# Five single moves in the instruction order of a retention and HGRN2 step

## The chip, the cores and the metric

The kernel runs on one core of a Trainium2 chip. The metric is the time of one execution in device microseconds, as the median of several runs.

## What is computed

One inference step of a hybrid decoder layer (depth 1): a prompt of 2048 tokens and eight decode rows of one token each, model width 1024. The normalised input is projected by w_in into eight groups of 512 columns; four of them feed a retention branch, four an HGRN2 branch. Each branch has four heads of 128 and runs a chunked recurrence; the outputs are normalised, gated and projected by w_out.

```
h = rmsnorm(x, norm_g)
p = h @ w_in
rq, rk, rv, rg, hq, hf, hi, hgate = split(p, 8)
# retention: rotary on rq, rk; fixed decay per head
o_ret, s_ret_new = chunked_decay_recurrence(rq, rk, rv, log_gamma, s_ret)
o_ret = head_rmsnorm(o_ret, ret_g) * silu(rg)
# HGRN2: forget gate from hf, key from 1 - gate
o_hg, s_hg_new = chunked_decay_recurrence(silu(hq), kin, hi, logf, s_hg)
o_hg = head_rmsnorm(o_hg, hg_g) * silu(hgate)
y = x + concat(o_ret, o_hg) @ w_out      # then the final rmsnorm
```

It returns the normalised y of the prompt and of the decode rows, and the new states of both branches for both.

## The kernel before

All large products are made from two parts of each operand, a high and a low one, with three matmuls (`three`, L348: high times high, high times low, low times high). The parts are made on chip: ACT (ScalarE) writes the high part, DVE (VectorE) the difference, both at L117 and L118 (`hi_lo`).

**Three main stages follow each other.** In the first, 24 token pairs (`v_pair(i, after)`, L383) run in three sets of eight. In each pair, a matrix product of blocks is made from seven smaller products (CHAIN, L355: A11·B11, A12·B21, S2·T2, S1·T1, S3·T3, S4·B22, A22·T4), each of twelve matmuls into a bank a, b or c; S and T are sums of blocks. The set number m says which weights are used. While set m−1 runs, the weights of set m are read (`wg_load`, at product 0 of pairs j = 2 to 5 of the set), multiplied with the eight decode rows (`wg_decode`, tile pgd, L590), summed to T1 to T4 and stored to memory (`wg_spool`: the sums in `w_sums` are four DVE instructions, the stores four DMAs by SP, SyncE, to ws1T). They are read back at j = 7 (`wg_fetch`) and split into high and low parts (`wg_split`) at the end of that pair and the start of the next one. In the third set the retention recurrence and the retention decode heads run beside the pairs (`r_*`, `d_load`, `d_mul`, `d_add`, `d_mm`): `d_load(hd)` loads a head's state dS and the broadcast values dv.

In the second stage the scan of HGRN2 runs in eight units (a half of the tokens and a head): the projection of a unit (`hgrn_proj`) is interleaved with the recurrence of the one before (`hgrn_rec`), whose steps stand in two lists, `levels` and `rest`, with a number that says at which share of the projection they are issued. `collect` copies the eight decode columns of q, k and f of each unit of the first half (df, dk, dq) and `d_pad(1)` pads the q of the four heads for the decode products (dqp). `side_at` lists steps beside a unit, with the unit's number and the share of it (4.1 is in unit 4).

In the third stage the output projection starts with four plain chunks (`py`, L1657) beside the tail of the last scan unit; the fill list gives each added step its share of the stage. Chunk pairs by seven products follow (`o_pair`); for the first, p0, `op_s12` (L1697) and `op_s34` (L1704) make sums of blocks (oS), `op_a` and `op_s23` split blocks and sums into high and low parts.

**What sets the order.** PE's order is the order in which the matmuls are written: a step in `after[n]` comes behind product n of a pair (0.5 is the middle of product 1). On the other engines a scheduler places the instructions, by their data, so a step that is written later may still be put ahead. `behind(f)` (L126) ties a step behind the last instructions so far of DVE, ACT and SP. All DMAs of the pairs go through SP's queue in its order, so a DMA that waits for data holds those behind it.

**The names in the steps.** pv3c is bank c of pair 3; B22h and B22l are the two parts of B22; wgr is the raw weight of a set; vo, rk, t are tiles of the rotation after a projection (`turn`, L360); pkt is the transpose of rk, par the scores of the retention; rq and rv are loaded from the stores qt_dram and v_dram; pah the scores in the scan; obh the normalised output of a head and poth its transpose; qqh and kh the scan's q and k.

Of the kernel before, what the change touches and what calls it, by code (L numbers as in the profile page):

```python
# [41 lines left out]
def step_kernel(ctx, tc, a, out):  # L42
# [83 lines left out]
    def behind(f):  # L126

        last = {}
        for i in reversed(nc.cur_bb.bb.instructions):
            if i.engine in (dve.engine, act.engine, sp.engine) and i.engine not in last:  # L130
                last[i.engine] = i
                if len(last) == 3:
                    break
        with ExitStack() as es:
            for i in last.values():
                es.enter_context(tc.issue_after(i))
            f()
# [383 lines left out]
    def wg_decode(n, k):  # L521
        if n not in pgd:
            pgd[n] = ps_o.tile([P, 256], F32, tag="o", name=f"pgd{n}")
        for kk in (k, k + 4):
            four(pgd[n], xs[:, kk], wr[kk].rearrange("p a b -> p (a b)"), kk == 0, kk == KT - 1)

    def wg_spool(n, k):
        for op, r in w_sums(wr[k], wr[k + 4]):
            sp.dma_start(w_sums_dram[n][op][:, k], r)
# [42 lines left out]
    def wg_split(op):  # L572
        h, l = Bop[op]
        for n, r in enumerate(wg_raw[op]):
            kk = slice(2 * n, 2 * n + 2)
            hi_lo(h[:, kk], l[:, kk], r)
# [252 lines left out]
    def d_load(hd):  # L829
        ty, h = divmod(hd, NH)  # L830
        S = rawp.tile([P, NB, P], F32, tag="raw", name=f"dS{hd}")
        vb = rawp.tile([P, NB, P], F32, tag="raw", name=f"dv{hd}")
        sp.dma_start(S, (a["state_ret"], a["state_hgrn"])[ty][0, :, h].rearrange("b d v -> d b v"))
        sp.dma_start(vb, vd_dram[ty, :, h * P : (h + 1) * P].partition_broadcast(P))
        dec["l", hd] = (S, vb)
# [19 lines left out]
    def d_pad(ty):  # L855
        if ty:
            x = pools["up"].tile([P, NH, 32], F32, tag="dqp", name="dqp")
        else:
            x = sm.tile([P, NH, 32], F32, tag="old", name="dqr", bufs=1)
        dve.tensor_copy(x[:, :, 8:32], zero.unsqueeze(1).to_broadcast([P, NH, 24]))  # L860
        dve.tensor_copy(x[:, :, 0:8], dq[:, ty * NH : ty * NH + NH])
        dec["q", ty] = x
# [41 lines left out]
    SPLIT_AT = 3  # L904
    for i in range(2, n_tok):
        after = {n: [] for n in range(7)}
        m, j = i // N_V + 1, i % N_V
        if N_V <= i < 2 * N_V:
            after[3.5 if i > N_V + 1 else 4.5 if i > N_V else 5.5] = [q_flip]
        if N_V < i <= 2 * N_V:  # L910
            after.setdefault(2.5 if i < N_V + 3 else 1.5 if i < 2 * N_V else 2, []).append(q_flip)
        if i in (N_V, 2 * N_V):
            after[4 if i == N_V else 1] += [lambda m=i // N_V: wg_decode_turn(m)]
        if i == 2 * N_V:
            r_begin()
        if i >= 2 * N_V:
            for n, f in r_steps(i - 2 * N_V).items():
                after.setdefault(n, []).extend(f)
        if same(i + 1):
            for op in ("S1", "S2", "S3", "S4"):  # L920
                sop[i + 1, op] = sop[i, op]
        elif i + 1 < n_tok:
            if not spooled(i + 1):
                after[1] += [lambda i=i: spread(i + 1)]
            tied = behind if i >= N_V - 1 else lambda f: f()
            late = 2 if same(i) else 0
            after[2 + late] += [
                lambda i=i, t=tied: t(lambda: tok_ops(i + 1)), lambda i=i, t=tied: t(lambda: s_split(i + 1, 0))
            ]
            after[4 + late // 2] += [lambda i=i, t=tied: t(lambda: s_split(i + 1, 1))]  # L930
        if i + 2 < n_tok and not same(i + 2):
            at = 5 if i % N_V > 2 else 2
            if same(i + 1):
                at = 6
            after[at] += [lambda i=i: tok_load(i + 2)]
        if i + 2 < N_V:
            after[1 if i == 2 else 2] += [lambda i=i: behind(lambda: stats_sum(i + 2, 0)), lambda i=i: stats_load(i + 2, 1)]
            after[4] += [lambda i=i: behind(lambda: stats_sum(i + 2, 1)), lambda i=i: stats_end(i + 2)]
            if i + 3 < N_V:
                after[5] += [lambda i=i: stats_load(i + 3, 0)]  # L940
        if N_V <= i + 1 < n_tok:
            after[4] += [lambda i=i: rot_load(i + 1)]
        if i == 2:
            after[3] += [lambda: behind(decode_values_out)]
            after[2] += [decode_spread]
        if m < 3:
            if 2 <= j < 6:
                after[0] += [lambda m=m, k=j - 2: wg_load(m, k)]
                after[4] += [lambda m=m, k=j - 2: wg_decode(m, k), lambda m=m, k=j - 2: wg_spool(m, k)]
            if j == 7:  # L950
                after[0] += [lambda m=m: behind(lambda: wg_decode_out(m))]
                for n, (_, op, _) in enumerate(CHAIN):
                    after[n] = [lambda m=m, op=op: wg_fetch(m, op)] + after[n]
        if i >= N_V - 1 and j in (7, 0) and i < n_tok - 1:
            for n, (_, op, _) in enumerate(CHAIN):
                if (n + SPLIT_AT) // 7 == (j + 1) % N_V:
                    after[3 if n == 6 else (n + SPLIT_AT) % 7] += [lambda op=op: behind(lambda: wg_split(op))]
        if i == 2 * N_V + 2:
            after[0] += [lambda: d_pad(0)]
        hd = i - 2 * N_V - 2  # L960
        if 0 <= hd < NH:
            after[2] += [lambda hd=hd: d_load(hd)]
        if 0 < hd < NH:
            after[5] += [lambda hd=hd: behind(lambda: d_mul(hd, 0))]
            after[6] += [lambda hd=hd: behind(lambda: d_add(hd))]
        if hd == 1:
            after[1] += [lambda: behind(lambda: d_mul(0, 0))]
            after[2] += [lambda: behind(lambda: d_add(0))]
        if 0 < hd <= NH:
            after[1 if hd > 1 else 3] += [lambda hd=hd: d_mm(hd - 1)]  # L970
        if N_V <= i < 2 * N_V:
            for n in range(12):
                for f, d in ((lambda n: behind(lambda: wo_pre_load(n)), 0), (lambda n: behind(lambda: wo_pre_split(n)), 2), (lambda n: behind(lambda: wo_pre_store(n)), 4)):
                    g = 7 + 4 * n + d
                    if g // 7 == i - N_V:
                        after[g % 7] += [lambda f=f, n=n: f(n)]
        if i == n_tok - 1:
            after[0] += [w_load]
            after[0] += [lambda: x_alloc(0), lambda: x_raw.update({(0, kp): x_load(0, kp) for kp in range(4)})]
            for kp, at in enumerate((1.5, 2.5, 3.5, 7)):  # L980
                if at > 6:
                    continue
                after.setdefault(at, [])
                after[at] += [lambda kp=kp: behind(lambda: x_split(0, kp, x_raw[0, kp]))]
            after[4] += [w_fetch]
        v_pair(i, after)
# [188 lines left out]
    def hgrn_rec(half, h, u):  # L1175
        name = f"h{half}{h}"
        hd = NH + h
# [148 lines left out]
        rest = [(0.02, begin), (0.13, t["u0"]), (0.28, t["u1"]), (0.43, t["o0"]), (0.47, t["o1"]),  # L1326
                (0.53, t["n0"]), (0.59, t["n1"]), (0.65, t["t0"]), (0.73, t["t1"]), (0.73, last)]
        if half == 0:
            levels.insert(0, (0.0, lambda: collect(h, u)))
        return levels, rest  # L1330

    def collect(h, u):
        for dst, key in ((dq, "q"), (dk, "k"), (df, "f")):
            dve.tensor_copy(dst[:, NH + h], u[key][:, HALF:])
# [88 lines left out]
        pool.dma_start(out["y_sample"], y[:NB])  # L1423

    side_at = []
    side_at.append((4.1, lambda: d_pad(1)))
    mm_at = {(1, 0, 3): [4], (1, 1, 1): [5], (1, 1, 3): [6], (1, 2, 1): [7]}
    for hd, at in zip(range(NH, 2 * NH), (5.1, 5.45, 6.1, 6.45)):
        steps = [d_load, lambda hd: d_mul(hd, 0), lambda hd: d_mul(hd, 1), d_add]
# [251 lines left out]
    def op_load(i):  # L1681
        oraw[i] = [rawp.tile([P, 8, P], F32, tag="raw", name=f"or{c}") for c in (2 * i, 2 * i + 1)]
        for c, r in zip((2 * i, 2 * i + 1), oraw[i]):
            sp.dma_start(r, o_dram[:, :, c * P : (c + 1) * P].rearrange("h p t -> p h t"))
# [35 lines left out]
    def op_a(i):  # L1720
        op_pair(i, oraw[i][0], "A11", "A12")

    def op_s23(i):
        op_pair(i, osum[i][0], "S2", "S3")
# [115 lines left out]
    for c in range(PLAIN):  # L1840
# [1 line left out]
    fill = place(fill, sorted([  # L1842
        *((0.04 * max(n - 1, 0), lambda s=s: behind(s)) for n, s in enumerate(wo1[2])),
        (0.03, wo1[1][2]), (0.07, wo1[1][3]),
        (0.2, d_norm), (0.6, t2_load), (0.65, lambda: op_load(p0)), (0.75, lambda: op_s12(p0)),
        (0.8, lambda: op_s34(p0)), (0.85, lambda: op_a(p0)), (0.9, lambda: op_s23(p0)),
        (0.95, t4_load), *((0.76 + 0.06 * n, lambda n=n: behind(lambda: t2_split(n))) for n in range(4)),
    ], key=lambda t: t[0]))
    merge(fill, [(0.57 * at, f) for at, f in levels], [(0.57 * at, f) for at, f in late], [(0.55 + 0.5 * at, f) for at, f in rest])
# [129 lines left out]
```

## Time and profile before

| what | value |
|---|---|
| median of 3 runs | 1036.96 us |
| lowest and highest run | 1035.46 and 1038.86 us |
| profiled execution | 1032.8 us |
| its span | 1031.0 us |
| granted TensorE clock in it | 0.999 |
| DMA, mean over the span | 248 GB/s |
| instructions in the trace | 21589 |

The profile page lists busy time by engine, the chain of work that ended last and the costliest groups of instructions. A row of the timeline reads: start, duration, engine, line, operation, out<-in, shape, count; in brackets stands the idle time of the engine just ahead and what ended it. In a table of waits the numbers are the total, the number of waits and the longest. In a table of windows each engine's busy time in the stretch stands with its instruction count, and at the end the granted clock, the DMA share and GB/s. PEld is PE's weight load, which overlaps its matmuls. SPq are the DMA issues of SP.

### The profile page before, as it was taken

To read this page: it belongs to the slowest core of one execution; us is meant where nothing else is said; L and a number is where in the kernel's file an instruction comes from. 1 tells how busy PE (TensorE), PEld (TensorE's weight loads), DVE (VectorE), ACT (ScalarE), POOL (GpSimd) and SP (SyncE) were. 2 spreads that over 40 slices of the span, in tenths; PEclk is the share of its full clock that TensorE was granted. 3 is DMA by queue.
4 is the path that set the end of the run, shared out by engine and by line. 5 is a ranking of instruction groups with operands and counts; after the bars stand their busy time and mean duration, and the time that the engine had idled before them with its cause. 6 is when DMAs were issued, how large, how long until landed. Compare 5 with 4: busy or idle time off the path is not lost.

```text
span 1031.0 us, 21589 instructions
## 1 busy us (share of the span) xinstructions
PE 1015.4 (98%) x8366; PEld 842.0 (82%) x8366; DVE 743.4 (72%) x1370; ACT 557.5 (54%) x1233; POOL 124.5 (12%) x231
## 2 busy tenths in 40 slices
PE   9999999999999999999999999999999999999997
PEld 7777778787778888888888899898888877888775
DVE  7886666888675885566666768768778676667886
ACT  7863345634434765545564756667556475443242
POOL 0200001000000101111111100111022112312122
PEclk9999999999999999999999999999999999999999
DMA  8699998778998974577776697655874496576652
GB/s 289 212 336 334 336 322 295 289 267 308 317 329 305 368 244 164 189 241 239 226 233 195 217 331 258 202 175 200 267 228 136 135 355 206 183 269 205 236 175 102
DMA packets 151271, 255.63 MB, mean 248 GB/s; under 512 B 11424, under 2 KB 79280, under 8 KB 151040
## 3 DMA queue, kind: packets, MB, share of 16 engines
q1 hardware_dynamic: 141408, 225.03, 64.9%
q0 software_dynamic: 7440, 24.76, 6.3%
q10 hardware_dynamic: 2320, 4.46, 1.1%
q8 instruction: 66, 1.08, 0.4%
q14 instruction: 37, 0.30, 0.1%
HBM read 166.51 MB, written 87.69 MB: 247 GB/s over the span
## 4 chain that ended last, share of the span: by engine, by line
PE 82%; DMA 10%; ACT 3%; DVE 2%; SPq 1%; issue 1%; POOL 0%; POOLq 0%; ACTq 0%; DVEq 0%
PE po L350 11%; PE pjqh L1024 8%; PE pjfh L1024 8%; PE py L1657 4%; DMA xn<-in_x_prompt 2%; PE pv L350 2%; PE plh L1242 2%; DMA wgr<-in_w 2%; PE par L731 1%; PE pur L738 1%; PE puh L1111 1%; PE por L744 1%; PE por L746 1%; DMA wg1B<-in_w 1%; DMA S<-s_dram 1%
## 5 line engine op out<-in xcount | busy, mean ns | idle before, releaser
L1222 ACT ACTIVATE kepth<-kh 128x1024 f32<-128x1024 f32 x24 | 25.5, 1060 | 63.0 <-DVE kh L1212 63.0
L1024 PE MATMUL pjfh<-xh,w_h 128*128 128x512 f32 (+2 forms) x160 | 59.5, 372 | 0.0
L1024 PE MATMUL pjqh<-xh,w_h 128*128 128x512 f32 (+2 forms) x160 | 58.8, 367 | 0.0
L1024 PE MATMUL pjfh<-xh,w_l 128*128 128x512 f32 (+2 forms) x160 | 55.7, 348 | 0.0
L1024 PE MATMUL pjqh<-xh,w_l 128*128 128x512 f32 (+2 forms) x160 | 55.7, 348 | 0.0
L1024 PE MATMUL pjfh<-xl,w_h 128*128 128x512 f32 (+2 forms) x160 | 55.6, 348 | 0.0
L1024 PE MATMUL pjqh<-xl,w_h 128*128 128x512 f32 (+2 forms) x160 | 55.6, 348 | 0.0
L1212 DVE TENSOR_TENSOR kh<-kh,fph 128x512 f32<-128x512 f32 x48 | 33.4, 695 | 22.6 <-PE plh L1242 17.8
L118 DVE TENSOR_TENSOR ab_l<-xr,ab_h 128x512 fp32r<-128x512 f32 (+1 forms) x40 | 37.5, 953 | 8.8 <-ACT ab_h L117 8.8
L769 DVE SCALAR_TENSOR_TENSOR obr<-por,omr,rg 128x128 f32<-128x128 f32 x64 | 18.0, 344 | 32.7 <-POOL omr L761 30.0
L759 ACT ACTIVATE obr<-por 128x128 f32<-128x128 f32 x64 | 16.9, 278 | 44.0 <-PE por L746 41.6
L117 ACT ACTIVATE ab_h<-xr 128x512 fp32r<-128x512 f32 (+1 forms) x40 | 32.4, 840 | 10.0 <-DVE xr L302 10.0
L409 ACT ACTIVATE vo<-vo 128x512 f32<-128x512 f32 x32 | 20.1, 629 | 28.8 <-DVE vo L403 13.1
L1024 PEld LDWEIGHTS pjqh<-xh,w_h 128*128 128x128 f32 x160 | 30.4, 190 | 4.8 <-issue 1.2
L1024 PEld LDWEIGHTS pjfh<-xh,w_h 128*128 128x128 f32 x160 | 30.2, 189 | 4.5 <-DVE qqh L1081 0.5
L1024 PEld LDWEIGHTS pjfh<-xh,w_l 128*128 128x128 f32 x160 | 30.1, 188 | 4.0
L1024 PEld LDWEIGHTS pjqh<-xh,w_l 128*128 128x128 f32 x160 | 30.1, 188 | 4.0
L1215 DVE TENSOR_TENSOR qqh<-qqh,fph 128x512 f32<-128x512 f32 x48 | 32.8, 683 | 0.0
L1024 PEld LDWEIGHTS pjqh<-xl,w_h 128*128 128x128 f32 x160 | 30.2, 189 | 2.9
L1024 PEld LDWEIGHTS pjfh<-xl,w_h 128*128 128x128 f32 x160 | 30.2, 189 | 2.7
L302 DVE SCALAR_TENSOR_TENSOR xr<-xr,g_in,rb 128x256 f32<-128x256 f32 x64 | 27.0, 479 | 6.3 <-issue 3.2
L1657 PE MATMUL py<-woh,oc_h 128*128 128x512 f32 x64 | 26.6, 415 | 0.0
(1840 smaller groups left out, 3360.1 us busy)
## 6 DMA issues: line engine op xcount, KB each, us to landing
xr<-a_dram SPq DMA_DIRECT2D x24, 512.0 KB
S<-s_dram SPq DMA_DIRECT2D x24, 512.0 KB
xn<-in_x_prompt SPq DMA_DIRECT2D x32, 256.0 KB
xr<-in_x_t SPq DMA_DIRECT2D x16, 512.0 KB
a_dram<-xr SPq DMA_DIRECT2D x16, 512.0 KB
s_dram<-S SPq DMA_DIRECT2D x16, 512.0 KB
wgr<-in_w SPq DMA_DIRECT2D x16, 512.0 KB
xr<-a_dram SPq DMA_DIRECT2D x32, 256.0 KB
```

What stands on the lines that cost most here:

```text
L117: act.activation(h, src, AF.Copy)
L118: dve.tensor_tensor(l, src, h.bitcast(F32), op=ALU.subtract)
L302: dve.scalar_tensor_tensor(r[:, k], r[:, k], g_in[:, kk : kk + 1], spread_to[i], op0=ALU.mult, op1=ALU.mult)
L350: pe.matmul(ps, xx, ww, start=(first and n == 0), stop=(last and n == 2), skip_group_check=more)
L409: act.activation(o, src, AF.Silu)
L769: dve.scalar_tensor_tensor(o[:, cc], po[:, h], ms[:, h : h + 1], rb_of[c, "g"][:, cc], op0=ALU.mult, op1=ALU.mult)
L1024: pe.matmul(ps, ww[:, kk], x[:, k, b0 : b0 + n], start=(k == 0 and i == 0), stop=(k == KT - 1 and i == 2),)
L1212: dve.tensor_tensor(kv[:, :, 0, :], kv[:, :, 0, :], two[:, :, 1:2].to_broadcast([P, nb, b]), op=ALU.mult)
L1215: dve.tensor_tensor(qv[:, :, 1, :], qv[:, :, 1, :], two[:, :, 0:1].to_broadcast([P, nb, b]), op=ALU.mult)
L1222: act.activation(ss[:, 512:], k[:, :HALF], AF.Copy)
L1242: pe.matmul(dst[32 * i : 32 * i + 32, c], kk, qq, start=True, stop=True)
L1657: pe.matmul(ps, o[:, kk], w[:, k % 4, i * 512 : (i + 1) * 512], start=(k == 0 and n == 0), stop=(k == KT - 1 and n == 2),)
```

## The change

Five places in the order change; no instruction is added or left out, and nothing is computed otherwise.

1. In pair 3 the decode products and the sums of the set's weights (`wg_decode`, `wg_spool`) come after product 5 instead of product 4.
2. In pairs 8 and 16 the split of B22 (n = 5 in CHAIN) comes in the middle of product 1 instead of after it.
3. The load of head 1's decode state, `d_load(1)` in pair 19, comes after product 3 and tied behind, instead of after product 2.
4. In the units of the first half `collect` moves from the start to 0.4, tied behind; `d_pad(1)` moves from 4.1 to 4.6.
5. In the third stage `op_s12`, `op_s34`, `op_a` and `op_s23` of the first pair move from 0.75, 0.8, 0.85 and 0.9 to 0.85, 0.88, 0.9 and 0.93.

```
-                after[4] += [lambda m=m, k=j - 2: wg_decode(m, k), lambda m=m, k=j - 2: wg_spool(m, k)]
+                after[5 if i == 3 else 4] += [lambda m=m, k=j - 2: wg_decode(m, k), lambda m=m, k=j - 2: wg_spool(m, k)]
...
                 if (n + SPLIT_AT) // 7 == (j + 1) % N_V:
-                    after[3 if n == 6 else (n + SPLIT_AT) % 7] += [lambda op=op: behind(lambda: wg_split(op))]
+                    after.setdefault(3 if n == 6 else 0.5 if n == 5 else (n + SPLIT_AT) % 7, []).append(
+                        lambda op=op: behind(lambda: wg_split(op))
+                    )
...
         if 0 <= hd < NH:
-            after[2] += [lambda hd=hd: d_load(hd)]
+            if hd == 1:
+                after[3] += [lambda: behind(lambda: d_load(1))]
+            else:
+                after[2] += [lambda hd=hd: d_load(hd)]
...
         if half == 0:
-            levels.insert(0, (0.0, lambda: collect(h, u)))
+            levels.append((0.4, lambda: behind(lambda: collect(h, u))))
...
-    side_at.append((4.1, lambda: d_pad(1)))
+    side_at.append((4.6, lambda: d_pad(1)))
...
-        (0.2, d_norm), (0.6, t2_load), (0.65, lambda: op_load(p0)), (0.75, lambda: op_s12(p0)),
-        (0.8, lambda: op_s34(p0)), (0.85, lambda: op_a(p0)), (0.9, lambda: op_s23(p0)),
+        (0.2, d_norm), (0.6, t2_load), (0.65, lambda: op_load(p0)), (0.85, lambda: op_s12(p0)),
+        (0.88, lambda: op_s34(p0)), (0.9, lambda: op_a(p0)), (0.93, lambda: op_s23(p0)),
```

On PE, in pair 3, the decode products (pgd, from the raw weights wgr and the decode rows pk) stood between the product of T3 and the one of B22:

```order
 L350 MATMUL pv3a<-T3l,s30h 128x512
 L350 MATMUL pv3a<-T3h,s30l 128x512
-L590 MATMUL pgd_919<-wgr_985,pk 8x256 x4
-L590 MATMUL pgd_919<-wgr_987,pk 8x256 x4
 L350 MATMUL pv3c<-B22h,s31h 128x512
 L350 MATMUL pv3c<-B22l,s31h 128x512
```

and now stand behind the twelve matmuls of B22, ahead of the product of T4:

```order
 L350 MATMUL pv3c<-B22l,s31h 128x512
 L350 MATMUL pv3c<-B22h,s31l 128x512
+L590 MATMUL pgd_919<-wgr_985,pk 8x256 x4
+L590 MATMUL pgd_919<-wgr_987,pk 8x256 x4
 L350 MATMUL pv3a<-T4h,ab_h 128x512
 L350 MATMUL pv3a<-T4l,ab_h 128x512
```

Eight matmuls moved past one product of twelve; this is all that moves on PE. In SP's queue the four stores of the sums (ws1T) of pair 3 thereby fall behind one store of values, two loads xr and two loads xn that stood behind them.

On DVE, in pair 8, the two halves of B22's low part stood behind the rotation of vo (five instructions) before:

```order
L118 TENSOR_TENSOR T3l<-T3l,T3h 128x1024 x2
L405 TENSOR_TENSOR vo_1851<-pv8b,s_8_1832 128x512
L370 TENSOR_TENSOR t_1853<-vo_1851,rot_1761 128x512
L373 TENSOR_TENSOR t_1854<-vo_1851,rot_1761 128x4x64
L374 SCALAR_TENSOR_TENSOR t_1854<-vo_1851,rot_1761 128x4x64
L375 TENSOR_TENSOR vo_1851<-t_1853,t_1854 128x512
L118 TENSOR_TENSOR B22l<-wg1B_1782,B22h 128x1024
L118 TENSOR_TENSOR B22l<-wg1B_1784,B22h 128x1024
L118 TENSOR_TENSOR T4l<-T4l,T4h 128x1024 x2
```

and now stand ahead of it:

```order
L118 TENSOR_TENSOR T3l<-T3l,T3h 128x1024 x2
L118 TENSOR_TENSOR B22l<-wg1B_1782,B22h 128x1024
L118 TENSOR_TENSOR B22l<-wg1B_1784,B22h 128x1024
L405 TENSOR_TENSOR vo_1855<-pv8b,s_8_1832 128x512
L370 TENSOR_TENSOR t_1857<-vo_1855,rot_1761 128x512
L373 TENSOR_TENSOR t_1858<-vo_1855,rot_1761 128x4x64
L374 SCALAR_TENSOR_TENSOR t_1858<-vo_1855,rot_1761 128x4x64
L375 TENSOR_TENSOR vo_1855<-t_1857,t_1858 128x512
L118 TENSOR_TENSOR T4l<-T4l,T4h 128x1024 x2
```

The same happens in pair 16, with rk in the place of vo and wg2B as the source of B22.

On DVE, in the third stage, the first sum of op_s12 (oS, from the loaded block or) stood ahead of the last scan products kh and qqh, which the head output obh follows:

```order
L1142 SCALAR_TENSOR_TENSOR obh_9837<-poh_9781,orsh_9799,v_9231 128x128 x4
L1170 COPY oldh_10067<-S_5655 128x128
L1701 TENSOR_TENSOR oS_2_10155<-or_10112 128x512
L1212 TENSOR_TENSOR kh_9109<-kh_9109,fph_9539 128x32x16
L1215 TENSOR_TENSOR qqh_9110<-qqh_9110,fph_9539 128x32x16
L1248 COPY_PREDICATED Abh_9571<-lmask,plh_9850 128x16x8
```

and now comes behind that obh and the two additions yc of the output (the lines of the change are five higher here):

```order
L1147 SCALAR_TENSOR_TENSOR obh_9924<-poh_9810,orsh_9828,v_9235 128x128 x4
L1635 TENSOR_TENSOR yc_9848<-py_9802,yc_9848 128x512
L118 TENSOR_TENSOR oc_l<-or_9935,oc_h 128x1024
L1635 TENSOR_TENSOR yc_9848<-py_9803,yc_9848 128x512
L1706 TENSOR_TENSOR oS_2_10247<-or_10112 128x512
L1217 TENSOR_TENSOR kh_9109<-kh_9109,fph_9539 128x8x64
```

So the last products kh and qqh and the second obh passed the first sum; the split op2A11l now also stands ahead of three of the four sums.

## The prediction

> **What bounds the kernel now.** I read the busy shares first, then the chain that ended last, then everything PE (TensorE) waited for, and last the timelines around the places that the five moves touch.
>
> ```profile
> PE 1015.4 (98%) x8366; PEld 842.0 (82%) x8366; DVE 743.4 (72%) x1370; ACT 557.5 (54%) x1233; POOL 124.5 (12%) x231
> ...
> PE 82%; DMA 10%; ACT 3%; DVE 2%; SPq 1%; issue 1%; POOL 0%; POOLq 0%; ACTq 0%; DVEq 0%
> ```
>
> PE is busy for 1015.4 of the span's 1031.0 us, and four fifths of the chain are PE. So only two things can shorten this kernel: fewer PE instructions, which the change does not bring, or shorter waits of PE. All of these that are long are in the table of PE's waits (total, times, longest):
>
> ```profile
> PE pgd L590 <- DMA wgr<-in_w: 2.4, 3, 1.0
> PE poth L1149 <- DVE obh L1142: 1.5, 2, 1.3
> PE pv8c L350 <- DVE B22l L118: 1.3, 1, 1.3
> ...
> PE par L731 <- DMA rq<-qt_dram: 0.8, 1, 0.8
> PE pah L1260 <- DVE dq L1334: 0.6, 1, 0.6
> ```
>
> They add up to 6.6 us, and most of that lies where the five moves are. That sum is about the most that could be won; what follows asks how much of each wait goes and what is late next.
>
> **Move 1, the decode products of pair 3.** PE at the present place:
>
> ```profile
> 91.74 0.39 PE L350 MATMUL pv3a<-T3h,s30l 128*128 128x512 f32 x1
> 93.16 0.62 PE L590 MATMUL pgd<-wgr,pk 128*8 128x256 f32 x8 [1.03 <-DMA wgr<-in_w]
> 94.60 0.62 PE L590 MATMUL pgd<-wgr,pk 128*8 128x256 f32 x8 [0.82 <-DMA wgr<-in_w]
> 95.15 0.50 PE L350 MATMUL pv3c<-B22h,s31h 128*128 128x512 f32 x1
> ...
> 114.66 1.05 PE L590 MATMUL pgd<-wgr,pk 128*8 128x256 f32 x16
> ...
> 135.18 1.33 PE L590 MATMUL pgd<-wgr,pk 128*8 128x256 f32 x16
> 135.89 0.12 PEld L590 LDWEIGHTS pgd<-wgr,pk 128*8 128x8 f32 x8 [0.59 <-DMA wgr<-in_w]
> ```
>
> From 91.74, the start of the last matmul ahead, to 95.15 PE spends 3.41 us; the same sixteen small matmuls took 1.05 us at 114.66, and the matmul ahead some 0.3, so about 2.05 us are lost. Afterwards a whole product stands in front of them: its twelve matmuls, at the pace of the one at 91.74 (0.39 each, overlapped to about 0.23), fill 2.7 us, so the first half is due near 94.7 and the second near 95.3. The operands were there by 93.16 and 94.60. At this place the whole 2.05 goes.
>
> What is late next are the same products in pairs 4 and 5, which stay where they are. PE reaches them 2 us sooner, and their weights come through DMA queues that are full:
>
> ```profile
> 93.00:115.00 22.00, 21.02 (x110) 16.32 (x114) 15.29 (x26) 8.55 (x17) 1.09 (x3) 1.00 1.03 388
> 115.00:136.00 21.00, 20.91 (x114) 16.20 (x106) 13.84 (x24) 9.51 (x18) 1.08 (x3) 1.00 0.96 340
> ```
>
> The last two columns are DMA share and GB/s. At a share of 1.03 nothing lands earlier because PE is earlier; at 0.96 some 0.04 × 21 = 0.8 us of room is left. In pair 5 the second half already waited (0.59 on the weight-load row; the group took 1.33, 0.28 more than in pair 4), so there the cover is used up, and in pair 4 it was at most some tenths to 2 us. Lower end: everything but 0.2 is given back. Upper end: 2.05. I take 1.2, the 2.05 less the full room of the queues: 2.05 − 0.8.
>
> The Trainium skill (DMA: Bandwidth & Descriptors, Specifications) puts the ceiling of the sixteen engines at 435 GB/s. By that rule the stretch at 388 GB/s is a tenth below it and would yield, and the term would be near 2.05; by the share of 1.03 it would be 0.2; the row is what I follow, and it does not decide for the second stretch.
>
> The stores of the sums (ws1T) now stand behind the loads xr and xn in SP's queue, and the weights of pair 4 right behind the stores; this is the slower rival below.
>
> **Move 2, the split of B22 half a product earlier (pairs 8 and 16).**
>
> ```profile
> 194.82 0.50 PE L350 MATMUL pv8c<-B22h,s71h 128*128 128x512 f32 x1
> 196.58 0.50 PE L350 MATMUL pv8c<-B22l,s71h 128*128 128x512 f32 x1 [1.25 <-DVE B22l L118]
> ...
> 188.78 1.23 DVE L118 TENSOR_TENSOR T3l<-T3l,T3h 128x1024 fp32r<-128x1024 f32 x1 [1.29 <-ACT T3h L117]
> 192.58 0.69 DVE L405 TENSOR_TENSOR vo<-pv8b,s 128x512 f32<-128x512 f32 x1 [2.57 <-DMA v_dram<-vo]
> ...
> 195.31 2.35 DVE L118 TENSOR_TENSOR B22l<-wg1B,B22h 128x1024 fp32r<-128x1024 f32 x2
> ```
>
> In pair 8 PE's second matmul starts 1.76 us after the first, where the step is some 0.34: 1.42 lost. DVE (VectorE) was idle for 2.57 us ahead of vo<-pv8b, waiting for a store. The order now puts both B22l pieces (2.35 us) in front of vo: they run from 190.0 to 192.4, so the hole hides them, vo is not later, and B22l is ready two microseconds before PE asks. Gain 1.4; vo still goes at 192.58 with the store, so PE's lead from move 1 shrinks in what hangs on vo (this lies in the bounds).
>
> In pair 16 there is no hole:
>
> ```profile
> 357.85 0.68 DVE L405 TENSOR_TENSOR rk<-pv16b,s 128x512 f32<-128x512 f32 x1
> ...
> 360.58 2.35 DVE L118 TENSOR_TENSOR B22l<-wg2B,B22h 128x1024 fp32r<-128x1024 f32 x2
> ...
> 362.70 0.60 PE L723 MATMUL pkt<-ident,rk 128*128 128x128 f32 x4
> ```
>
> The rotation of rk, which ends as B22l begins, now comes 2.3 us later, near 362.9, while PE transposes rk at 362.70. That is a new wait of 0.3, and up to 1.0 if PE arrives with the lead of the moves before and DVE does not follow; I take 0.5. B22l was not waited for here, so nothing is won. Move 2 nets −0.9.
>
> **Move 3, the decode state of head 1 (pair 19).** SP's issues:
>
> ```profile
> 439.56 0.38 SPq L833 DMA_DIRECT2D dS<-in_state_ret  x1
> 440.69 0.37 SPq L834 DMA_DIRECT2D dv<-vd_dram  x1
> ...
> 443.21 0.33 SPq L718 DMA_DIRECT2D rq<-qt_dram  x1
> ...
> 453.40 1.22 DVE L842 TENSOR_TENSOR dv<-dv,dk 128x1024 f32<-128x1024 f32 x1
> 456.02 0.69 DVE L370 TENSOR_TENSOR t<-pv19a,rot 128x512 f32<-128x512 f32 x1 [1.41 <-PE pv19a L350]
> ```
>
> rq, for which PE waited 0.8 (the table), is queued behind dS and dv; now rv and rq are issued before both. The wait goes: −0.8 (bounds 0 and −0.85, as rq could still be held by its buffer). dv is some 3 us later instead; its first user at 453.40 is followed by 1.41 us of idle DVE, so up to 1.4 costs nothing and the rest moves a rotation that PE asks for much later. I put no price on it.
>
> **Move 4, the copies of decode columns.**
>
> ```profile
> 702.19 0.42 DVE L1083 TENSOR_TENSOR qqh<-qqh,fh 128x256 f32<-128x256 f32 x1
> 702.53 0.16 DVE L1334 COPY dq<-qqh 128x8 f32<-128x8 f32 x1
> ...
> 706.51 0.17 DVE L861 COPY dqp<-dq 128x32 f32<-128x32 f32 x1
> ...
> 725.80 1.10 PE L1149 MATMUL poth<-ident,obh 128*128 128x128 f32 x4 [0.23 <-DVE obh L1142]
> ```
>
> The table puts PE's 0.6 down to the copy dq, but PE reads qqh, which ends just as the copy does (702.61). The copy itself is not on the path; only df and dk, of the same size and further ahead, are, at no more than 0.16 each: −0.2 (bounds 0 and −0.56). The two pad copies (dqp) now stand directly in front of the obh group that PE already waits 0.23 for: at most 2 × 0.17, so +0.3. Net +0.1. The other copies fall where DVE idles.
>
> **Move 5, the sums of the out stage.**
>
> ```profile
> 866.31 0.69 DVE L1701 TENSOR_TENSOR oS<-or 128x512 f32<-128x512 f32 x1 [3.37 <-DMA or<-o_dram]
> ...
> 869.95 1.12 DVE L1142 SCALAR_TENSOR_TENSOR obh<-poh,orsh,v 128x128 f32<-128x128 f32 x4
> ...
> 870.35 1.10 PE L1149 MATMUL poth<-ident,obh 128*128 128x128 f32 x4 [1.28 <-DVE obh L1142]
> ...
> 888.75 1.06 ACT L117 ACTIVATE op2S2h<-oS 128x1024 fp32r<-128x1024 f32 x1 [1.90 <-PE py L1657]
> ```
>
> The first sum holds DVE for 3.37 us until a load lands, and the scan's products queue behind it up to obh, for which PE then waits 1.28. With the sum moved behind obh and two yc, DVE can start that chain sooner by as much as the idle and the sum are long, 3.37 + 0.69 = 4.1 us, less what its own inputs, PE's scores plh, still hold it; the wait needs a third of that: −1.3 (bounds −0.5, if the scores come late, and −1.45). The sums are needed at 888.75 and would end some 8 us before; that hides them.
>
> **The sum.** −1.2 − 0.9 − 0.8 + 0.1 − 1.3 = −4.1 us. The profiled execution took 1032.8 us (span 1031.0 and 1.8 around it), 4.2 under the median of the runs, 1036.96; the waits are a fixed piece of the program, so I apply the difference to the median: 1032.9. A measurement of this kernel tells 0.3%, 3.1 us, from no change.
>
> **Rivals.**
> (a) The queues take move 1 back: the wait goes on at the products of pairs 4 and 5, and the full queues around pair 16 do the same there. Then move 1 is worth 0.2 and pair 16 costs 1.0: −0.2 − 0.4 − 0.8 + 0.1 − 1.3 = −2.6, that is 1034.4, within 0.3%. For it: the shares of 1.03 and 0.96 and the 0.59 already waited in pair 5. Against: pair 4 showed no wait. A milder form, a wait that keeps half of its length in moves 3 and 5 because the releaser named is not the last one, gives the same figure.
> (b) Slower, by SP's queue at pair 3. The stores of the sums wait for DVE, and the weights of pair 4 stand behind them:
>
> ```profile
> 105.36 1.44 SPq L517 DMA_DIRECT2D wgr<-in_w  x2
> ...
> 96.38 0.69 DVE L503 TENSOR_TENSOR wgr<-wgr 128x512 f32<-128x512 f32 x1
> ...
> 106.43 0.69 DVE L405 TENSOR_TENSOR vo<-pv4b,s 128x512 f32<-128x512 f32 x1 [5.64 <-PE pv4b L350]
> ```
>
> If the sums slipped through DVE's idle 5.64 us to 106.4, the weights would be issued about 7 later and PE would stand at pair 4 for that and move 1's lead, 8 us or more: −4.1 + 8 = +3.9, 1040.9. It decides from 7.2 us of lateness on (3.1 + 4.1). Against it: DVE began the first sum at 96.38, 1.2 us after the products had ended (94.60 + 0.62), so it had other work ahead of them, and products that end near 95.6 hardly move the sums.
>
> **How the numbers follow.** The forecast has a chance of 0.63, (a) 0.31, (b) 0.06. The prices' own bounds add up to −5.8 at the best end (2.05, 1.1, 0.85, 0.3 and 1.45) and to −0.8 at the other (0.2, 0.4, 0 and 0.5, less 0.3), which is 1031.2 and 1036.2. A median of few runs, which here spread over 3.4 us, can lie half a us off, so the range is 1030.6 to 1036.4; it holds the forecast and nearly all of (a), and about one in ten lies beyond each end. Faster by over 0.3% means below 1033.85: 0.63; within 0.3%: 0.31; slower: 0.06.
>
> **What would show it.** Right: in the waits of PE after, B22l, rq and the obh of 1.28 are gone, pgd has lost its two waits near 93 us, and a new one of a few tenths stands at pkt in pair 16. The forecast is wrong if pgd waits as long as before in pairs 4 and 5, which is (a), if SP waits for wgr ahead of its weight loads, which is (b), or if a wait with the same matmul only gets another releaser.

## The result and the profile after

| | median | runs | lowest to highest |
|---|---|---|---|
| before, as known at the prediction | 1036.96 us | 3 | 1035.46 to 1038.86 |
| before, with the runs beside the change | 1035.69 us | 8 | 1032.25 to 1038.86 |
| after | 1029.74 us | 8 | 1027.5 to 1033.54 |

The ratio is 0.9942 with a 95% interval of 0.9923 to 0.9962: faster by 6.0 us (3.9 to 8.0). The forecast was 4.1 us and 1032.9, in a range from 1030.6 to 1036.4. The direction was right, the gain too small, and the time lies 0.9 us below the range. The profiled execution of after took 1029.99 us, 2.8 less than the profiled one of before. So the two profiles show half of what the medians show, and that is the first thing to explain.

The page of after, the shares of busy time:

```profile
PE 1015.1 (99%) x8366; PEld 842.1 (82%) x8366; DVE 744.2 (72%) x1370; ACT 557.7 (54%) x1233; POOL 124.8 (12%) x231
```

PE's waits after (total, times, longest):

```profile
PE pgd L590 <- DMA wgr<-in_w: 1.9, 4, 0.7
...
PE pdt L1397 <- DVE do L1393: 0.7, 1, 0.7
PE prs L288 <- POOL rs_all L114: 0.6, 1, 0.6
PE pah L1265 <- DVE fph L1208: 0.5, 1, 0.5
```

PE does the same work in the same busy time. B22l, rq and the long wait for obh have left the table; pdt is new, prs is up from 0.2; pgd is shorter but has four waits in place of three. PE's timeline in the stretch of pairs 3 to 5:

```profile
94.08 0.39 PE L350 MATMUL pv3c<-B22h,s31l 128*128 128x512 f32 x1
94.40 1.07 PE L590 MATMUL pgd<-wgr,pk 128*8 128x256 f32 x16
95.40 0.50 PE L350 MATMUL pv3a<-T4h,ab_h 128*128 128x512 f32 x1
...
104.44 0.43 PE L288 MATMUL prs<-ident,rs_all 128*128 128x128 f32 x2 [0.58 <-POOL rs_all L114]
...
113.87 0.62 PE L590 MATMUL pgd<-wgr,pk 128*8 128x256 f32 x8 [0.25 <-DMA wgr<-in_w]
...
134.44 0.62 PE L590 MATMUL pgd<-wgr,pk 128*8 128x256 f32 x8 [0.45 <-DMA wgr<-in_w]
135.74 0.62 PE L590 MATMUL pgd<-wgr,pk 128*8 128x256 f32 x8 [0.68 <-DMA wgr<-in_w]
```

In pair 3 nothing is waited for any more, and PE is 2.6 us ahead of before at the first product behind it (95.40 against 98.02). Behind the pgd of 135.74 the lead is 0.15 us: it went at prs (0.75), at pair 4 and twice at pair 5. That is the give-back of the first rival, but not by its queues alone, for prs waits for POOL and not for a load. The windows (last, DMA share and GB/s) are as full as they were:

```profile
93.00:115.00 22.00, 21.17 (x116) 15.38 (x115) 14.97 (x26) 8.91 (x17) 1.08 (x3) 1.00 1.00 371
115.00:136.00 21.00, 19.86 (x101) 15.59 (x99) 14.11 (x25) 8.92 (x17) 1.08 (x3) 1.00 0.98 346
```

SP and ACT show a part of its way that the prediction had only as a far case:

```profile
102.47 0.94 SPq L263 DMA_DIRECT2D xn<-in_x_prompt  x2
103.50 2.25 SPq L529 DMA_DIRECT2D ws1T<-wgr  x4
...
106.78 1.20 SPq L517 DMA_DIRECT2D wgr<-in_w  x2
...
SPq L263 <- ACT xn L269: 3.1, 3, 2.7
...
101.24 0.60 ACT L390 ACTIVATE s<-pv4a 128x512 f32<-128x512 f32 x1 [2.18 <-PE pv4a L350]
101.73 0.62 ACT L269 ACTIVATE xn<-xn 128x512 f32<-128x512 f32 x1
...
103.69 0.69 POOL L114 TENSOR_TENSOR rs_all<-rs_all,mhalf 128x2 f32<-128x2 f32 x1
```

SP stood 2.7 us for the buffer of xn, whose squares ACT now makes behind s<-pv4a, so the weights of pair 4 were issued at 106.78, later than before (105.36) although PE is earlier. The statistics for prs come from the same squares, through POOL, whose last step ends at 104.38, just ahead of prs (104.44). That this is why prs waits was not tried by itself, but a step of 0.7 us stands there in each of the seven profiles that hold move 1, and in none of the others.

The other places after, in their order:

```profile
190.66 2.35 DVE L118 TENSOR_TENSOR B22l<-wg1B,B22h 128x1024 fp32r<-128x1024 f32 x2
192.94 0.69 DVE L405 TENSOR_TENSOR vo<-pv8b,s 128x512 f32<-128x512 f32 x1
...
195.20 0.50 PE L350 MATMUL pv8c<-B22h,s71h 128*128 128x512 f32 x1
195.54 0.39 PE L350 MATMUL pv8c<-B22l,s71h 128*128 128x512 f32 x1
...
361.72 0.63 PE L723 MATMUL pkt<-ident,rk 128*128 128x128 f32 x4
...
449.24 1.06 PE L731 MATMUL par<-rq,kT 128*128 128x128 f32 x8
...
862.54 0.69 DVE L1217 TENSOR_TENSOR kh<-kh,fph 128x512 f32<-128x512 f32 x1 [1.37 <-PE plh L1247]
...
867.14 0.60 PE L1154 MATMUL poth<-ident,obh 128*128 128x128 f32 x4
...
909.55 0.69 DVE L1800 TENSOR_TENSOR xro<-xro,os 128x512 f32<-128x512 f32 x1 [4.19 <-DMA xro<-in_x_prompt]
...
914.97 0.24 PE L1397 MATMUL pdt<-ident,do 64*128 64x64 f32 x1 [0.69 <-DVE do L1393]
```

B22l fills DVE's hole, and PE's second matmul follows the first after 0.34 us instead of 1.76. In pair 16 pkt comes 0.28 later than its neighbours, the new wait of a few tenths. par follows without a gap. The chain to obh starts when plh lets it (862.54), and poth takes 0.60 instead of 1.10: its four transpositions had waited for DVE one by one, too. The new wait at pdt stands behind a load: xro<-in_x_prompt holds DVE 4.19 us, where it held it 2.40 before; its addition comes 1.95 us earlier than before, PE by then 3.7.

### The profile page after: what moved, and what is told of

It reads as the page before. It is cut to its first block, busy times and chain, and to the rows that moved or that the text cites. A ratio compares the mean times of both kernels' runs of the same rounds, so it can differ in the third digit from the quotient of the medians.

```text
span 1028.1 us, 21593 instructions
## 1 busy us (share of the span) xinstructions
PE 1015.1 (99%) x8366; PEld 842.1 (82%) x8366; DVE 744.2 (72%) x1370; ACT 557.7 (54%) x1233; POOL 124.8 (12%) x231
```

## The experiments

A ratio stands with its 95% interval. "Clock" is the mean over a kernel's runs of the granted TensorE clock. Each row has 6 to 12 runs, and 11 to 35 of the kernel before, taken beside them.

| kernel | median us | before beside it | ratio | clock |
|---|---|---|---|---|
| before again | 1034.23 | 1034.81 | 0.9991 (0.9972 to 1.0009) | 0.9971 |
| move 1 alone | 1033.15 | 1034.81 | 0.9978 (0.9959 to 0.9997) | 0.9976 |
| move 2 alone | 1034.12 | 1035.69 | 0.9989 (0.9973 to 1.0006) | 0.9969 |
| move 5 alone | 1033.54 | 1034.81 | 0.9988 (0.9967 to 1.0010) | 0.9962 |
| moves 2 to 5 | 1032.38 | 1034.81 | 0.9957 (0.9936 to 0.9978) | 0.9974 |
| moves 1, 2 | 1032.88 | 1035.13 | 0.9974 (0.9960 to 0.9988) | 0.9981 |
| moves 3, 4, 5 | 1032.00 | 1035.13 | 0.9970 (0.9953 to 0.9986) | 0.9976 |
| all five again | 1028.83 | 1035.51 | 0.9934 (0.9911 to 0.9958) | 0.9983 |
| pgd of pair 3 earlier | 1039.02 | 1035.69 | 1.0030 (1.0014 to 1.0046) | 0.9943 |
| pgd after product 5 everywhere | 1029.88 | 1035.69 | 0.9954 (0.9936 to 0.9973) | 0.9986 |
| pgd after product 5 in pairs 2 to 5 | 1029.30 | 1035.69 | 0.9944 (0.9925 to 0.9963) | 0.9984 |
| pgd after product 5 in pairs 3 to 5 | 1028.39 | 1035.51 | 0.9939 (0.9916 to 0.9961) | 0.9987 |

Four theories are tried. They are: A, the gain beyond the profiles' 2.9 us is the chance of single runs; B, typical executions of before wait longer for wgr than the profiled one; C, a wait costs its length and no more; D, long waits also bring down the clock. C and D came up after the profile of move 5 alone.

**The kernel before, again.** No edit.

> The kernel before, unchanged, for a second profile. The two profiles at hand differ by 2.9 us of span, the medians by 5.95 us. Theory A (the difference of the medians beyond 2.9 us is the spread of single runs): ratio 1.000, and PE's waits in its profile add up to about what the first profile shows, pgd 2.4 us, all within 1 us. Theory B (typical executions of the kernel before wait longer for the weights wgr than the profiled one did): ratio 1.000, but where the profiled execution takes 1035 us or more, its pgd row is 4 us or more instead of 2.4.

Measured: 0.9991, and 1031.99 us in its profiled run; pgd 3.3 us in five waits. Its profiled run was the shortest of its twelve, so it could not decide B.

**Move 1 alone.**

```
-                after[4] += [lambda m=m, k=j - 2: wg_decode(m, k), ...]
+                after[5 if i == 3 else 4] += [lambda m=m, k=j - 2: wg_decode(m, k), ...]
```

> Move 1 alone (decode products and sums of pair 3 after product 5). Theory A: PE gains 2.2 us near 92 us and gives all but 0.2 back by pair 8, at the transposition prs and at pgd of pairs 4 and 5; ratio 0.9995 to 1.0005. Theory B: the gain is kept in typical runs, ratio 0.997 (3 us).

Measured: 0.9978, which is 1.7 us by the medians. In its trace PE gains 2.3 us at pair 3 and is at +0.35 us against the first profile of before by pair 6, so against that profile it is given back in full, as A said; in the median it is not. The interval reaches from B's 0.997 to A's 0.9995, so the ratio does not decide.

**Moves 2 to 5, without move 1.** The change less the line above.

> Moves 2 to 5 without move 1. Theory A: the same as all five, ratio 0.994 to 0.996 with its profile 2.5 to 3.5 us below before, since move 1 brought 0.2. Theory B: ratio 0.997 (3 us less gain than all five, 0.9942).

Measured: 0.9957, which is A's ratio, but the interval holds B's 0.997 as well; and the profile, at 1032.38 us, is 0.4 us under the first of before, where A had 2.5 to 3.5. This trace has two waits of its own at pair 16 (total, times, longest):

```profile
PE pkt L723 <- DVE rk L375: 1.7, 1, 1.7
PE pv16a L350 <- ACT s L390: 1.1, 1, 1.1
```

ACT had stood 2.92 us for a load shortly before, and with B22l ahead of rk that reached pkt, by the order of the rows; it was not tried by itself. This is what the prediction had as 0.5 and at most 1.0 in pair 16; in the other four profiles with move 2 it is 0.3 to 0.5.

**Move 5 alone.** The third stage's line alone.

> Move 5 alone (first sums of the out stage later). Both theories: PE's wait for obh near 870 us goes (1.4 us), and a new wait at the transposition pdt near 917 us (0.8 us) takes part of it back if the later sums cause it; then the ratio is 0.999 to 0.9995. If pdt's wait is not there, it belongs to another move and the ratio is 0.9985.

Measured: 0.9988 (its interval holds both answers). The wait of over a us for obh near 870 goes. At pdt the step is 0.3. It is 0.7 with all five and without move 1, but nothing in the second profile of all five and in that of moves 3 to 5, and 0.5 in one profile of the kernel before: it changes from execution to execution, and these traces do not put it down to a move. The surprise of this trace is elsewhere. Pair 3 is as before here, and PE's timeline and the windows behind it (granted clock, DMA share and GB/s at the end) read:

```profile
93.22 0.62 PE L590 MATMUL pgd<-wgr,pk 128*8 128x256 f32 x8 [1.28 <-DMA wgr<-in_w]
94.75 0.62 PE L590 MATMUL pgd<-wgr,pk 128*8 128x256 f32 x8 [0.91 <-DMA wgr<-in_w]
95.30 0.80 PE L350 MATMUL pv3c<-B22h,s31h 128*128 128x512 f32 x1
95.90 0.63 PE L350 MATMUL pv3c<-B22l,s31h 128*128 128x512 f32 x1
96.32 0.63 PE L350 MATMUL pv3c<-B22h,s31l 128*128 128x512 f32 x1
```

```profile
90.00:95.00 5.00, 2.81 (x25) 1.52 (x23) 4.10 (x6) 2.50 (x4) 0.00 (x0) 1.00 0.87 304
95.00:98.60 3.60, 3.60 (x16) 2.62 (x9) 3.51 (x5) 2.20 (x6) 0.00 (x0) 0.53 1.03 419
```

From 95.25 us the records grant half the clock for 3.41 us; a matmul takes 0.63 instead of 0.39 and starts 0.43 after the last instead of 0.23. Half of 3.41 is 1.7 us, beside 2.2 us of the two waits in front of it. The first profile of before has no such stretch; both of these profiles have the usual one at the end, when PE has run out of work, which costs nothing. From here on theory D stood beside C.

**The decode products of pair 3 one product earlier still**, in the kernel before.

```
-                after[4] += [lambda m=m, k=j - 2: wg_decode(m, k), ...]
+                after[3 if i == 3 else 4] += [lambda m=m, k=j - 2: wg_decode(m, k), ...]
```

> The kernel before, with the decode products of pair 3 one product earlier still (after product 3), so that PE waits there some 2.7 us longer. Theory C (a wait costs its length): PE loses 2.7 us more near 92 us and gets up to 1.1 of it back in pairs 4 and 5, where the weights then are less late; ratio 1.0015 to 1.0026 (1.6 to 2.7 us), clock of the runs as in the kernel before, 0.997 on average. Theory D (long waits close together also make the clock gate grant half the clock for some 3.4 us, as in the profile of move 5 alone from 95.25 us on, for 1.7 us more): the profile shows a half clock behind these products, the mean clock of the runs is lower by 0.0010 or more, and the ratio is 1.003 to 1.0045.

Measured: 1.0030 and a clock of 0.9943, 0.0024 under the 0.9967 of before beside it. The ratio is at the edge between the two, the clock is not. PE's timeline and a window of this trace:

```profile
93.40 0.89 PE L590 MATMUL pgd<-wgr,pk 128*8 128x256 f32 x8 [4.12 <-DMA wgr<-in_w]
...
96.45 0.63 PE L350 MATMUL pv3a<-T3l,s30h 128*128 128x512 f32 x1
```

```profile
95.00:100.00 5.00, 5.00 (x18) 3.29 (x12) 3.90 (x5) 1.30 (x5) 0.00 (x0) 0.50 1.01 406
```

The half clock lasts 6.83 us here, twice 3.41. At the first product of B22 PE is 5.7 us later than in the first profile: 2.9 of that is more waiting (4.12 and 0.59 against 1.03 and 0.82), the rest mostly the clock. By C it would have been the 2.9 alone. So a wait that was made longer brought the half clock with it, and the clock of 11 of the 12 runs is 0.996 or less.

**Move 2 alone.** Pairs 8 and 16, the two lines of the split.

> Move 2 alone (B22's split half a product earlier in pairs 8 and 16). Both theories: the wait for B22l in pair 8 goes (1.4 us), a wait of 0.3 to 1.9 at the transposition of rk in pair 16 comes (0.3 with all five moves, 1.9 with moves 2 to 5); ratio 0.9985 to 1.0005.

Measured: 0.9989; the wait for B22l gone (a step of −1.4 in PE's starts), pkt at +0.3. As expected.

**More profiles of the kernel before**, four in all, no edit.

> The kernel before, one more profile, to see where half-clock stretches fall in it. Theory D: if its time is 1035 us or more, there is a stretch of about 3.4 us at half clock in the middle of the program, right behind a wait of PE of over a us, most likely behind pgd in pair 3 or at B22l in pair 8. Theory C: a time of 1035 us or more comes with longer waits at full clock.

> The same as the one before it: one more profile of the kernel before.

> One more profile of the kernel before. Theory D: a half-clock stretch ahead of the tail, if there is one, stands right behind pgd in pair 3 or B22l in pair 8; a time of 1037 us or more has two or three. Theory C: no opinion.

> The same as the one before it: one more profile of the kernel before.

Measured: 1035.59, 1033.87, 1034.99 and 1038.28 us. With the two profiles above, pgd's waits in the kernel before add up to 2.4, 3.3, 3.0, 3.5, 4.2 and 4.3 us, of which the first profile has the least. That is B's mechanism, though weaker than B had it: at 1035.59 us they are 3.0 and not 4. The first of the four, PE around B22l and the window behind it:

```profile
196.31 0.50 PE L350 MATMUL pv8c<-B22l,s71h 128*128 128x512 f32 x1 [1.57 <-DVE B22l L118]
...
197.73 0.63 PE L350 MATMUL pv8c<-B22h,s71h 128*128 128x512 f32 x1
```

```profile
197.00:201.00 4.00, 4.00 (x13) 3.10 (x12) 4.00 (x6) 1.35 (x3) 0.00 (x0) 0.57 0.73 239
```

The second has none ahead of the tail, the third has one behind pgd in pair 3 (waits 1.95 and 0.63; 3.41 us from 96.21). The fourth, the longest, has two: its waits, and the windows of both places:

```profile
PE pgd L590 <- DMA wgr<-in_w: 4.3, 4, 3.3
PE poth L1149 <- DVE obh L1142: 1.8, 2, 1.6
```

```profile
94.00:101.00 7.00, 5.60 (x25) 3.12 (x26) 5.40 (x7) 3.21 (x6) 0.00 (x0) 0.52 1.02 390
...
875.00:879.00 4.00, 4.00 (x12) 3.14 (x12) 1.81 (x2) 2.53 (x5) 0.54 (x1) 0.57 0.32 131
```

So pgd in pair 3, B22l in pair 8 and obh near 870 each have a half clock behind them in one execution or another, and pgd's wait itself goes up to 3.3 us in place of 1.0. D had named the first two; the third it had not.

**Moves 1 and 2 against moves 3, 4 and 5.**

> Moves 1 and 2 alone, which take away the two waits behind which a half-clock stretch was seen (pgd in pair 3 in the profile of move 5 alone, B22l in pair 8 in a profile of the kernel before). Theory D: mean clock of the runs as with all five, 0.9980 or more, hardly a run at 0.996 or less; time 2.5 to 3.5 us below before although the profiles' ledger gives these two moves 1.0 to 1.5; ratio 0.9966 to 0.9976. Theory C: 1.0 to 1.5 us, ratio 0.9986 to 0.9990, mean clock as in the kernel before, 0.9968.

> Moves 3, 4 and 5 alone. The ledger gives them 1.0 for rq, 1.4 to 1.9 for obh, less 0.2 for the pads and up to 0.8 at pdt: about 2 us, ratio 0.998. Theory D: the waits of pair 3 and pair 8 stay and with them their half-clock stretches: mean clock 0.9970 or less, several runs at 0.996 or less, the spread of the runs as wide as before's. Theory C has no opinion on the clock.

Measured: moves 1 and 2 0.9974, clock 0.9981, one run of twelve at 0.996 or less: as D had it for the clock and the ratio, although the interval reaches to C's 0.9988. Their one profile, too, has a half-clock stretch, behind the obh that they leave alone (3.41 us from 872.83):

```profile
871.53 1.10 PE L1151 MATMUL poth<-ident,obh 128*128 128x128 f32 x4 [2.19 <-DVE obh L1144]
```

Moves 3 to 5 brought 0.9970 with a clock of 0.9976 and three runs at 0.996 or less. D had said 0.998 and 0.9970; it had left out that move 5 takes a place away, too. In the profile the stretch stands behind pgd in pair 3 (waits 2.89 and 0.61; 3.41 us from 94.89). The two halves, 2.3 and 3.1 us by their medians, add up to 5.4, about the whole. The clock of 0.9976 is a miss for D here, and 0.9970 is more gain than the ledger of either theory.

**All five again.** No edit.

> All five moves once more. Theory C (waits cost their length alone; the excess over the profiles' 2.9 us is chance): ratio nearer to 0.997, mean clock of the runs as in the kernel before (0.9967). Theory D (the moves also take away half-clock stretches that typical runs of the kernel before have and its profiled run had not): ratio 0.994 to 0.996, mean clock 0.998, no run at 0.996 or less.

Measured: 0.9934, clock 0.9983, no run under 0.998: D. The profiled run, 2.7 us under the first of before, has no half clock ahead of the tail.

**The decode products after product 5 in more pairs** (all five moves besides, B22's split moved in pair 8 alone), three kernels. The first moves them everywhere, as below; the second in pairs 2 to 5 (`5 if i < N_V else 4`), the third in pairs 3 to 5 (`5 if 3 <= i < N_V else 4`).

```
-                after[5 if i == 3 else 4] += [...]
+                after[5] += [...]
-                    after.setdefault(3 if n == 6 else 0.5 if n == 5 else (n + SPLIT_AT) % 7, []).append(
+                    after.setdefault(3 if n == 6 else 0.5 if n == 5 and i == N_V else (n + SPLIT_AT) % 7, []).append(
```

> All five moves, and the decode products after product 5 in every pair that has them, not only in pair 3; B22's split moves in pair 8 alone. If move 1's gain is given back only because the products of pairs 4 and 5 stay where they are: pgd's waits (1.9 us with all five) go to under 0.5, pkt's 0.3 goes, and the time is 1.5 to 2.5 us under all five, ratio 0.992. If the full DMA queues hold the stretch, another wait for a load takes their place by pair 8 and the ratio stays at 0.994.

> As the version before it, but the products move only in pairs 2 to 5 and stay after product 4 in the second and third set. The same two answers: 0.992 or 0.994; against that version the difference tells whether the second set's products (pgd waited 0.4 to 0.6 near 259 us in two of the profiles) matter: under 0.6 us either way.

> All five moves, with the decode products after product 5 in pairs 3, 4 and 5, not in pair 2 (where that made PE wait 1.0 to 1.7 us at pv2c for ACT), and B22's split moved in pair 8 alone. If pair 2 alone spoilt the two versions before: pgd's waits in pairs 4 and 5 (1.5 us) go, prs's waits for rs_all (0.7 each) may come in pairs 4 and 5; 0.5 to 1.5 us under all five, ratio 0.993. If the queues hold the stretch: the same as all five within 0.5 us.

Measured: 0.9954, 0.9944 and 0.9939, all level with the change itself (0.9942 and 0.9934). pgd's waits in pairs 4 and 5 go, and others take their place. With pair 2 moved, a wait at pv2c (the first trace, PE):

```profile
72.32 0.50 PE L350 MATMUL pv2c<-B22h,s21h 128*128 128x512 f32 x1 [1.73 <-ACT p L390]
```

and in all three PE's waits at prs triple (the last of them):

```profile
PE prs L288 <- POOL rs_all L114: 1.7, 3, 0.6
PE pgd L590 <- DMA wgr<-in_w: 1.4, 3, 0.6
```

None of them beats the change. So what holds PE next in pairs 4 and 5 is no load: it is prs, whose wait of 0.6 us is the same in every one of these traces, however early PE comes.

## Why the prediction was wrong

**The step that failed** is the one from the profiled execution to the median: "the waits are a fixed piece of the program, so I apply the difference to the median". They are not fixed, in two ways. They vary in length from execution to execution, and the profiled one lay at the short end (pgd 2.4 us, against 3.0 to 4.3 in the other five profiles of before); and behind a long one the clock may fall to half for 3.4 us or 6.8. The six profiled executions of before took 1034.6 us in the mean, 1.8 more than the first, and the two of the change 1030.0: that is 4.6 between the profiles, where the first two showed 2.8. The runs bear out the second beyond the single traces. Of the 95 runs of the kernel before beside the experiments, 36 have a clock of 0.998 or more and a median of 1033.2 us, 59 have less and a median of 1036.0, and the 30 at 0.996 or less a median of 1037.3. Of the 14 runs of the change none is under 0.997, and their median is 1029.6. Against the upper group that is 3.6 us, close to the profiles' 2.8; against all 95 (1035.1) it is 5.5. The difference of the mean clocks, 0.9969 and 0.9982, is worth 0.0013 × 1035 = 1.3 us. That is a rough price: the mean also counts the half clock at the end of a run, which costs nothing and is all that the profiled run of the change lost (0.998).

The prediction has no term for the clock: its windows have 1.00, and I took that for a property of the kernel. The Trainium skill (TensorE: Matmul & The Clock Gate, HAM oscillation) says that PE's idle gaps of over about 3.4 us make the gate halve the clock. By that rule only the 4.12 us of the experiment would have done it. The traces agree on the half; they differ on the gap, and the measurement decides: a single 1.57, or 1.28 and 0.91 in sequence, was enough.

**Term by term.** PE's matmuls are the same in all kernels, so a place's price in an execution is how much later or earlier PE leaves a stretch than in the first profile. The table gives the mean of the profiles without and with each move (nine or ten without, four or five with; the experiment with the longer wait and the three last kernels left out). Stretches are in the first profile's us; of the one from 200 to 400 only the step at pkt is counted.

| move, stretch | without | with | difference | forecast |
|---|---|---|---|---|
| 1, 89 to 150 | +1.3 | +0.4 | −0.9 | −1.2 |
| 2, pair 8, 150 to 200 | +0.2 | −1.4 | −1.6 | −1.4 |
| 2, pair 16, at pkt (step) | 0 | +0.7 | +0.7 | +0.5 |
| 3, 400 to 470 | 0 | −1.1 | −1.1 | −0.8 |
| 4, 470 to 860 | +0.2 | +0.5 | +0.3 | +0.1 |
| 5, 860 to 890 | +0.3 | −2.0 | −2.3 | −1.3 |
| 5, 890 to the end | +0.1 | +0.3 | +0.2 | 0 |

The +0.7 is the mean of 0.3, 0.5, 0.3, 0.3 and 1.9. The differences add up to −4.7; the forecast's −4.1 is short of that by 0.6, and by 1.0 in move 5 alone. The medians give −5.5 to −6.7, so that 1 to 2 us of the gain have no place in these few profiles.

- Move 1: the place was read rightly, and so was that there is a give-back up to pair 5, but it went further than the 0.8 that I took: against the first profile, nothing is left, as in the first rival. And 0.7 of it, at prs, was not foreseen. What the move is worth, 0.9, lies in the executions in which the weights come later (pgd's longest wait 2.0, 2.9 or 3.3 us), and those the first profile did not show; that 0.9 lies near the 1.2 is luck. Whether the queues would have yielded these runs do not show: the share stayed at 1.00 and 0.98, but what came next at PE was in good part prs, which waits for no load.
- The slower rival: its mechanism took place in small. SP stood 2.7 us ahead of the stores and the weights came 1.4 us later; PE waited a quarter of a us for them in pair 4. It was far from the 7.2 us it needed.
- Move 2: right in pair 8; in pair 16 right in sign and size, with one execution of 1.9.
- Move 3: right; dv's delay hurt nothing.
- Move 4: right that the copy was not what PE waited for: pah waits 0.5 still, in the same place, now put down to fph. Hardly anything of the gain of 0.2 came (0.6 to 0.5), the cost did (a step of 0.2 at poth near 725).
- Move 5: the term mis-sized. I took the wait in front of the first of four transpositions, 1.28, while each of the four waits for its own obh; with them the stretch gives 2.0 in the profiles, and 2.3 with the executions that have a half clock there. The give-back at pdt was not foreseen: where it stands, DVE's load xro comes earlier by less than PE does. Two of the five profiles with the move have none.
- The base: 1036.96 was a median of three; the eight runs beside the change have 1035.69, the 95 later ones 1035.1. Of the 3.2 us by which the time was missed, 1.3 are that base, for which the range had half a us, and 1.9 the gain, which at 6.0 is beyond the best end of the prices, 5.8. That end, and the 6.6 us of waits as "about the most that could be won", were sums over one execution.

**Why a wait brings the half clock in one execution and not in another.** In the main it depends on where the wait falls. In the clock records of the traces, every stretch at full clock that ends ahead of the tail is a whole number of 3.413 us long (26 of them, 88.75 us, in four traces; 56, 191.15 us, in one), as the stretches at half clock are. So each trace divides into slots of 3.413 us, which begin at another point of the program in each execution. Slots of the trace of move 5 alone, at pair 3 and at pair 8:

```profile
91.83:95.24 3.41, 1.22 (x17) 0.23 (x16) 3.41 (x7) 1.87 (x3) 0.00 (x0) 1.00 0.92 344
95.25:98.66 3.41, 3.41 (x12) 2.68 (x9) 3.32 (x4) 1.95 (x5) 0.00 (x0) 0.50 1.03 419
...
194.23:197.64 3.41, 2.51 (x13) 1.61 (x11) 2.79 (x6) 2.05 (x3) 0.00 (x0) 1.00 0.48 193
197.64:201.06 3.42, 2.27 (x10) 1.92 (x11) 3.42 (x4) 2.48 (x5) 0.00 (x0) 1.00 0.30 93
```

and of the first profile of before, at pair 3:

```profile
90.48:93.90 3.42, 2.27 (x16) 1.15 (x14) 2.82 (x4) 1.17 (x2) 0.00 (x0) 1.00 0.83 274
93.90:97.31 3.41, 2.71 (x17) 1.91 (x18) 3.32 (x6) 3.16 (x6) 0.00 (x0) 1.00 1.03 419
```

The number behind the slot's length is PE's busy time. In the first slot PE is idle for 2.19 us, and the next one runs at half. B22l's wait of 2.0 us in the same trace is cut in two by a slot's end, 0.90 and 1.15, and so are the two waits of the first profile, 1.15 and 0.70; nothing follows them. In all eighteen traces, ahead of the tail, each half clock begins at the end of a slot in which PE was idle for 1.57 us or more. All five full-clock slots with 1.96 us or more have one behind them, and three of the nine between 1.57 and 1.92.

Not settled: what tells these nine apart, and why the weights come later in one execution than in another.

## What to carry to other kernels

One profile sizes the waits of one execution. Where the runs of a kernel spread by more than a move is worth, look at their granted clocks beside their times before applying a difference from one profile to a median: a wait of PE of some 1.6 us or more can cost about its length once more, by the clock, when it falls into one slot. And a wait in front of a group of matmuls that each need their own operand is longer than the idle time in front of the first.

## What the runs showed of the hardware that was not expected

The granted clock fell to half, for 3.41 us or 6.83, behind waits of PE from 1.57 us on (or two of 1.28 and 0.91 close together), in eight stretches ahead of the tail in the eighteen traces, always behind one of three places and always from the end of a slot of 3.413 us with 1.57 us or more of idle PE; the matmul's step went from 0.23 to 0.43 us. The matching figure of whole runs is a median of 1036.0 us for the kernel before where the mean clock is below 0.998, against 1033.2 where it is 0.998 or more.
